# One one-hot product with 128 places per expert, and one shared third tile of down for the leftover tokens

## The chip, the cores and the metric

The kernel runs on one core of one Trainium2 chip. The metric is the device time of one execution in microseconds; it is given as the median of several runs, with the lowest and the highest. One further execution was recorded by the profiler; the rows below come from it.

## The reference, cut to what matters

The program is one block of an encoder: attention and a short convolution on the normed input, added to the residual, then a layer of 16 experts, then a last norm. The change lies in the layer of experts. Each expert chooses its own tokens:

```python
cap = EC_CAPACITY_FACTOR * L // N_EXPERTS           # 2 * 528 // 16 = 66 tokens
g, idx = lax.top_k(aff.T, cap)                      # per expert
xg = hs[idx]                                        # (16, 66, 1024)
a = jnp.einsum('ecd,edf->ecf', xg, w_gate)          # 1024 -> 2048
u = jnp.einsum('ecd,edf->ecf', xg, w_up)
y = jnp.einsum('ecf,efd->ecd', jax.nn.silu(a) * u, w_down)   # 2048 -> 1024
y = y * g[..., None]
out = jnp.zeros((L, D), y.dtype).at[idx.reshape(-1)].add(y.reshape(-1, D))
```

All is float32. The three weight matrices of an expert have 24 MiB together, those of all experts 384 MiB. 66 tokens are 64 and 2 more, and these two are what the change is about.

## The kernel before

After attention and convolution (to about 315 us) and the routing (to about 350 us) comes the loop over experts, L1024 to L1057, in an order written out by hand (`order3`, a manual schedule). Weights are streamed: 384 loads of 1 MiB, issued by SyncE in the order of their use (`pump`, L752) into a ring of 20 buffers (`raw`); `nextw` (L950) takes the oldest buffer for TensorE and issues loads for those that are free.

Expert e has 16 steps of gate and up. A step is 64 matmul instructions on one load (`prod`, L957, weights stationary, the 66 tokens moving; every float32 product is two instructions). After every second step stand two more pieces of work: one piece of to_tokens for the results of expert e-2 (L1038, from the third expert on), and one piece of down for expert e-1 (L1040). So 8 times per expert TensorE does 128 instructions of gate or up, one to_tokens and one `down_piece`.

`down_piece` (L976) takes a load of w_down and multiplies it with the hidden values H (2048 x 66, 16 tiles of 128 x 66), H stationary and weights moving, in four column strips of 32. Three strips hold three groups of tokens, which begin at `GR = (0, 32, 34)`: tokens 0 to 31, 32 to 63 and 34 to 65, so that the third group repeats 30 tokens for the sake of the last two. Groups 0 to 2 are rows 0 to 95 of the three PSUM banks of y (banks 0 and 1); what the fourth strip (rows 96 to 127, one bank per group) gives is the second half of the columns for the odd inner tiles and is added later.

`down_rows` (L989) reads y when an expert's down is complete: ScalarE scales with the gate and rounds to the two-part form's first part (yh, L996), VectorE takes the difference as the second part (yl, L997), ScalarE brings the fourth strip over in three passes (L1000), VectorE adds (L1001), ScalarE and VectorE split again (L1002, L1003). GpSimd makes the one-hot matrix oh (L1005), 96 places x 512 tokens, from the token numbers in `at96`; the repeated 30 places have the number 0 and match nothing.

`to_tokens` (L1008) sends results back to token order with two products, oh times yh and oh times yl, each 96 places x 128 tokens x 512 columns, into the one bank of T, and VectorE adds T to `acc` (L1015).

`at96` is made in the routing: the product with `sel` (L922) spreads numbers and gates of the 66 tokens over 96 places. It stands between the gather of the first expert's rows and `spin(5)`, products without use that TensorE does until the first expert can begin.

PSUM has eight banks. A pool lays its tags into banks in the order in which they are first asked for: in the pool of the loop T has bank 0, G banks 1 and 2, U banks 3 and 4, y banks 5 to 7. The pools of the tail, opened when that pool is closed, lay ys0 and ys1 into banks 0 and 1 and the six places of `bank()` into banks 2 to 7 (in the order 2, 7, 3, 4, 5, 6 as they are asked for). A tile of theirs waits until the tiles that lay in its bank have been read for the last time (`reuse_waits="tile"`).

The tail (from L1059) is no longer in an order by hand: a planner orders the instructions of each engine when the program is built, by their place in the text and by what is ready. The last expert's down runs there with weights stationary: eight steps of 64 instructions into ys0 and ys1 (L1100), each followed by one to_tokens for expert 14 (L1101); then the last expert's own products to token order (L1079), the sums, the last norm and the stores.

## Time and profile before

| | |
|---|---|
| median of 3 runs | 1372.51 us (1372.21 to 1373.56) |
| the profiled execution | 1373.22 us, its span 1371.4 us |
| TensorE busy | 1272.6 us (93% of the span) |
| VectorE, ScalarE, GpSimd busy | 29%, 17%, 13% |
| read from HBM | 427.19 MB, 315 GB/s over the span |
| chain that ended last | TensorE 78%, DMA 7%, VectorE 6% |

The page gives busy times, 40 equal slices of the span, the DMA queues and the chain of work that ended last; further views give the same for any stretch, line or tile. The engines are TensorE (PE; its weight loads into the array stand apart as PEld), VectorE (DVE), ScalarE (ACT), GpSimd (POOL) and SyncE (SP, with its queue SPq). L957 is line 957 of the kernel. A name as y<-raw,H says what is written and what is read.

### The profile page before, as it was taken

The page shows a single profiled execution, that of the slowest core. Times are in us where ns is not written, and L with a number is a line of the kernel's source. Part 1 is how long each engine was busy: PE and PEld are TensorE (multiplying, and loading weights), DVE is VectorE, ACT ScalarE, POOL GpSimd, SP SyncE. Part 2 cuts the span into 40 slices and gives each one's busy share as a digit, 9 for nine tenths or more (in the row PEclk, how much of TensorE's full clock was granted, in tenths as well). Part 3 has the DMA queues.
Part 4 walks back from the last instruction along what each step waited for, and adds up shares of the span by engine and source line. Part 5 has one row for each costly group of instructions (what it writes and reads, how often), then busy time and mean ns, then how long its engine had stood idle before and what let it go on. Part 6 is the DMA issues. An engine that isn't in the chain of part 4 may idle for free.

```text
span 1371.4 us, 47094 instructions
## 1 busy us (share of the span) xinstructions
PE 1272.6 (93%) x22328; PEld 931.3 (68%) x22328; DVE 391.0 (29%) x669; ACT 232.1 (17%) x431; POOL 175.3 (13%) x139
## 2 busy tenths in 40 slices
PE   7897989997879999999999999999999999999996
PEld 6677989995666666666666666666666666565664
DVE  6876776545000111112111112111111111121114
ACT  4455444322000101011010101001010101010112
POOL 2734441331100000000000000000000000000002
PEclk8899889998899999999999999999999999999998
DMA  7311211294999999999999999999999999999994
GB/s 208 93 32 31 62 32 62 94 383 171 337 335 401 396 398 404 391 407 393 406 399 403 385 386 399 392 399 390 399 386 403 393 388 405 382 402 397 407 369 157
DMA packets 142883, 434.51 MB, mean 317 GB/s; under 512 B 13201, under 2 KB 37777, under 8 KB 142689
## 3 DMA queue, kind: packets, MB, share of 16 engines
q1 hardware_dynamic: 139936, 423.49, 80.8%
q0 software_dynamic: 2752, 8.00, 1.9%
q8 instruction: 175, 2.87, 0.9%
q14 instruction: 20, 0.16, 0.0%
HBM read 427.19 MB, written 4.26 MB: 315 GB/s over the span
## 4 chain that ended last, share of the span: by engine, by line
PE 78%; DMA 7%; DVE 6%; issue 4%; ACT 3%; POOL 2%; SPq 0%; DVEq 0%; ACTq 0%; POOLq 0%
PE y L984 21%; PE G L957 17%; PE U L957 17%; PE T L1014 5%; PE pj L274 5%; PE pj L304 3%; DMA raw<-in_w_gate 3%; DMA raw<-in_w_up 3%; PE ys L957 1%; PE pj L344 1%; PE y L986 1%; ACT qsw L365 1%; PE sc L430 1%; PE T L969 1%; ACT p L441 1%
## 5 line engine op out<-in xcount | busy, mean ns | idle before, releaser
L984 PE MATMUL y<-raw,H 128*32 128x512 f32 x2160 | 338.4, 599 | 2.0 <-issue 2.0
L986 PE MATMUL y<-raw,H 128*32 128x512 f32 x720 | 333.6, 599 | 1.5 <-issue 1.5
L957 PEld LDWEIGHTS U<-X,raw 128*64 128x64 f32 x8192 | 249.9, 139 | 66.4 <-issue 51.2
L957 PEld LDWEIGHTS G<-X,raw 128*64 128x64 f32 x8192 | 249.1, 138 | 59.7 <-issue 52.3
L957 PE MATMUL U<-X,raw 128*64 128x66 f32 x8192 | 261.7, 224 | 23.6 <-issue 18.1
L957 PE MATMUL G<-X,raw 128*64 128x66 f32 x8192 | 260.8, 224 | 17.3 <-issue 14.6
L1015 DVE TENSOR_TENSOR acc<-acc,T 128x512 f32<-128x512 f32 x112 | 76.9, 687 | 598.1 <-PE T L1014 598.1
L984 PEld LDWEIGHTS y<-raw,H 128*32 128x32 f32 x2160 | 79.9, 109 | 187.0 <-issue 172.8
L1052 ACT ACTIVATE H<-G 128x264 f32<-128x264 f32 x64 | 21.5, 388 | 595.1 <-PE G L957 595.1
L915 POOL DMA_INDIRECT xg<-hn_rows,idxT x16 | 16.3, 1017 | 699.4 <-PE T L969 680.1
L986 PEld LDWEIGHTS y<-raw,H 128*32 128x32 f32 x720 | 69.4, 110 | 7.0 <-issue 6.9
L274 PE MATMUL pj<-xh,wl 128*128 128x264 f32 x320 | 69.3, 300 | 0.0
L274 PE MATMUL pj<-xl,wh 128*128 128x264 f32 x320 | 67.7, 294 | 0.0
L274 PE MATMUL pj<-xh,wh 128*128 128x264 f32 x320 | 67.2, 293 | 0.0
L996 ACT ACTIVATE yh<-y,at 96x512 fp32r<-96x512 f32 x15 | 10.3, 684 | 281.9 <-PE y L986 281.9
L1014 PE MATMUL T<-yh,oh 96*128 96x512 f32 x112 | 55.8, 498 | 0.0
L274 PEld LDWEIGHTS pj<-xh,wl 128*128 128x128 f32 x320 | 52.9, 201 | 0.1
L274 PEld LDWEIGHTS pj<-xl,wh 128*128 128x128 f32 x320 | 52.5, 199 | 0.0
L274 PEld LDWEIGHTS pj<-xh,wh 128*128 128x128 f32 x320 | 52.2, 198 | 0.0
L1005 POOL TENSOR_SCALAR oh<-tok,at 96x512 fp32r<-96x512 int16 x15 | 23.6, 1573 | 171.4 <-PE T L1014 171.4
L1014 PE MATMUL T<-yl,oh 96*128 96x512 f32 x112 | 44.4, 397 | 0.6 <-issue 0.6
L1054 DVE TENSOR_TENSOR H<-H,U 128x264 f32<-128x264 f32 x64 | 24.4, 423 | 70.8 <-PE U L957 70.8
(226 smaller groups left out, 1201.3 us busy)
## 6 DMA issues: line engine op xcount, KB each, us to landing
raw<-in_w_up SPq DMA_DIRECT2D x128, 1024.0 KB, 18.8
raw<-in_w_gate SPq DMA_DIRECT2D x126, 1024.0 KB, 19.1
raw<-in_w_down SPq DMA_DIRECT2D x126, 1024.0 KB, 19.1
raw<-in_w_in SPq DMA_DIRECT2D x24, 512.0 KB, 5.3
raw<-in_w_out SPq DMA_DIRECT2D x8, 512.0 KB, 4.1
hn_rows<-raw SPq DMA_DIRECT2D x4, 512.0 KB, 4.8
raw<-in_w_gate POOLq DMA_DIRECT2D x2, 1024.0 KB, 8.0
out<-raw SPq DMA_DIRECT2D x4, 512.0 KB, 3.1
```

Of the source, the lines that this page charges most:

```text
L274: nc.tensor.matmul(o[:, hf * 512:hf * 512 + HALF], a[:, c], b[:, HS[hf]], start=c == 0 and n == 0, stop=c == DC - 1 and n == 2)
L304: nc.tensor.matmul(o[:, hf * 512:hf * 512 + HALF], a[:, k, i * P:(i + 1) * P], b[:, HS[hf]], start=k == 0 and n == 0, stop=k == 3 and n == 2)
L344: nc.tensor.matmul(o, a[:, ts], b, start=c == 0 and n == 0, stop=c == DC - 1 and n == 2)
L915: nc.gpsimd.indirect_dma_start(out=xg, out_offset=None, in_=hn2_d, in_offset=bass.IndirectOffsetOnAxis(ap=idxT[:CAP, e:e + 1], axis=0))
L957: nc.tensor.matmul(out[64 * q:64 * q + 64], w[:, c0 + 64 * q:c0 + 64 * q + 64], x, start=first, stop=last, skip_group_check=True)
L984: nc.tensor.matmul(y[32 * g:32 * g + 32, ob], H[:, 2 * d + ci, GR[g]:GR[g] + 32], w[:, o:o + 512], start=d == 0 and r != 1, stop=d == 7 an ...
L986: nc.tensor.matmul(y[96:128, r], H[:, 2 * d + 1, GR[r]:GR[r] + 32], w[:, 1536:2048], start=d == 0, stop=d == 7, skip_group_check=True)
L1005: nc.gpsimd.tensor_scalar(oh, tok, at96[:96, e:e + 1], None, op0=ALU.is_equal)
L1014: nc.tensor.matmul(po, oh[:, t * P:(t + 1) * P], b[:, hfs], start=n == 0, stop=n == 1)
L1015: nc.vector.tensor_tensor(acc[:, t, hfs], acc[:, t, hfs], po, op=ALU.add)
L1052: nc.scalar.activation(dst, src, AF.Silu)
L1054: nc.vector.tensor_tensor(dst, dst, src, op=ALU.mult)
```

## The change

- The two parts of an expert's first 64 tokens become the upper and the lower half of one tile of 128 places (`rows`), so that one product per piece sends both back; oh has 128 places, each token number standing twice (`atp` instead of `at96`).
- The last two tokens of every expert are collected: after each half of gate and up VectorE copies their hidden values into two of the 32 columns of HL (one HL for even, one for odd experts), GpSimd clears those of two experts before. The third group of `down_piece` multiplies HL instead of H. Its rows of y (64 to 95, and the third bank of the fourth strip) are started once, at expert 0, and go on adding over all 15 experts, each expert at its own two rows.
- y is now one tile for the whole loop, asked for before all others of its pool, instead of a new one per expert.
- `down_rows` reads 64 rows of y instead of 96 and has two passes for the fourth strip instead of three. At the end of the loop the shared 32 rows are read once, in the same way (`two_parts`), as a second product (`oh_l`, `rows_l`) for the 8 to_tokens of the tail, which still have two products each.
- In the routing `sel` is made anew, a second product spreads the leftover tokens' numbers and gates over 32 rows of 16 x 2, and `own` picks for each row its own expert's (`atl`).

```diff
@@ -771,12 +769,23 @@
     nc.vector.tensor_scalar(anti, jq, 0.0, None, op0=ALU.is_equal)
 
 
-    jg = hp.tile([P, 3, 32], I32, name="jg")
-    for k in range(3):
-        nc.gpsimd.iota(jg[:, k], pattern=[[-1, 32]], base=-GR[k], channel_multiplier=1)
-    sel = hp.tile([P, 3, 32], F32, name="sel")
-    nc.vector.tensor_scalar(sel, jg, 0.0, None, op0=ALU.is_equal)
-    nc.vector.memset(sel[:, 2, :64 - GR[2]], 0.0)
+
+    sel = hp.tile([P, 3, 64], F32, name="sel")
+    jg = hp.tile([P, 2, 64], I32, name="jg")
+    nc.gpsimd.iota(jg, pattern=[[0, 2], [-1, 64]], base=0, channel_multiplier=1)
+    nc.vector.tensor_scalar(sel[:, 0:2], jg, 0.0, None, op0=ALU.is_equal)
+    jl = hp.tile([P, 32, 2], I32, name="jl")
+    nc.gpsimd.iota(jl, pattern=[[0, 32], [-1, 2]], base=-64, channel_multiplier=1)
+    nc.vector.tensor_scalar(sel[:, 2], jl.rearrange("p a b -> p (a b)"), 0.0, None, op0=ALU.is_equal)
+    own = hp.tile([64, 2, NE], F32, name="own")
+    for k in range(2):
+        jo = hp.tile([32, NE], I32, name=f"jo{k}")
+        nc.gpsimd.iota(jo, pattern=[[-2, NE]], base=0, channel_multiplier=1)
+        jf = hp.tile([32, NE], F32, name=f"jf{k}")
+        nc.vector.tensor_scalar(jf, jo, 0.0, None, op0=ALU.is_ge)
+        nc.vector.tensor_scalar(own[32 * k:32 * k + 32, 0], jo, 2.0, None, op0=ALU.is_lt)
+        nc.vector.tensor_tensor(own[32 * k:32 * k + 32, 0], own[32 * k:32 * k + 32, 0], jf, op=ALU.mult)
+        nc.vector.tensor_copy(own[32 * k:32 * k + 32, 1], own[32 * k:32 * k + 32, 0])
     lg = sc()
 
@@ -918,13 +927,18 @@
 
     xg = gather(0)
 
-    pp96 = pj()
-    nc.tensor.matmul(pp96[:96, :2 * NE], sel[:CAP].rearrange("p a b -> p (a b)"),
+    ppl = pj()
+    nc.tensor.matmul(ppl[:, :2 * NE], sel[:CAP, 0:2].rearrange("p a b -> p (a b)"),
                      vals2[:CAP].rearrange("p a b -> p (a b)"), start=True, stop=True)
+    nc.tensor.matmul(ppl[:64, 512:512 + 2 * NE], sel[:CAP, 2], vals2[:CAP].rearrange("p a b -> p (a b)"),
+                     start=True, stop=True)
     spin(5)
-    at96 = const.tile([P, 2 * NE], F32, name="at96")
+    atp = const.tile([P, 2 * NE], F32, name="atp")
+    atl = const.tile([64, 2], F32, name="atl")
     last = const.tile([P, 2], F32, name="last")
-    nc.vector.tensor_copy(at96[:96], pp96[:96, :2 * NE])
+    nc.vector.tensor_copy(atp, ppl[:, :2 * NE])
+    nc.vector.tensor_tensor(own, own, ppl[:64, 512:512 + 2 * NE].rearrange("p (a e) -> p a e", e=NE), op=ALU.mult)
+    nc.vector.reduce_sum(atl, own, axis=AX.X)
     nc.vector.tensor_copy(last[:CAP], vals2[:CAP, :, NE - 1])
     pump(NRAW, nc.gpsimd)
@@ -941,7 +955,10 @@
     ps2 = psm.enter_context(tc.tile_pool(name="ps2", bufs=1, space=PSUM, reuse_waits="tile"))
     NF = DFF // P
     HS = [wk.tile([P, NF, CAP], F32, name=f"H{i}") for i in range(2)]
-    tok = wk.tile([96, 512], mybir.dt.int16, name="tok")
+    HL = [wk.tile([P, NF, 32], F32, name=f"L{i}") for i in range(2)]
+    for h_ in HL:
+        nc.gpsimd.memset(h_, 0.0)
+    tok = wk.tile([P, 512], mybir.dt.int16, name="tok")
     nc.gpsimd.iota(tok, pattern=[[1, 512]], base=NMETA, channel_multiplier=0)
 
@@ -973,45 +990,62 @@
     def new_x():
         return wk.tile([P, DC, CAP], F32, name="X", tag="X", bufs=2)
 
-    def down_piece(y, H, d):
+    y = ps2.tile([P, 3, 512], F32, name="y")
+
+    def down_piece(e, d):
+
 
 
         w = nextw()
+        H, Hl = HS[e % 2], HL[e % 2]
+
+        def st(f, g):
+            return Hl[:, f] if g == 2 else H[:, f, 32 * g:32 * g + 32]
+
+        def first(g):
+            return d == 0 and (g < 2 or e == 0)
+
+        def final(g):
+            return d == 7 and (g < 2 or e == NE - 2)
+
         for r in range(3):
             ob, ci = ((0, 0), (0, 1), (1, 0))[r]
             o = ci * 1024 + ob * 512
             for g in range(3):
-                nc.tensor.matmul(y[32 * g:32 * g + 32, ob], H[:, 2 * d + ci, GR[g]:GR[g] + 32], w[:, o:o + 512],
-                                 start=d == 0 and r != 1, stop=d == 7 and r != 0, skip_group_check=True)
-            nc.tensor.matmul(y[96:128, r], H[:, 2 * d + 1, GR[r]:GR[r] + 32], w[:, 1536:2048], start=d == 0, stop=d == 7,
+                nc.tensor.matmul(y[32 * g:32 * g + 32, ob], st(2 * d + ci, g), w[:, o:o + 512],
+                                 start=first(g) and r != 1, stop=final(g) and r != 0, skip_group_check=True)
+            nc.tensor.matmul(y[96:128, r], st(2 * d + 1, r), w[:, 1536:2048], start=first(r), stop=final(r),
                              skip_group_check=True)
 
-    def down_rows(y, e):
-
-        gate = at96[:96, NE + e:NE + e + 1]
-        yh = wk.tile([96, D], FR, name="yh", tag="yh")
-        yl = wk.tile([96, D], FR, name="yl", tag="yl")
-        tmp = wk.tile([96, 512], F32, name="tmp", tag="tmp")
-        a, b = slice(0, 512), slice(512, D)
-        nc.scalar.activation(yh[:, a], y[:96, 0], AF.Copy, scale=gate)
-        nc.vector.scalar_tensor_tensor(yl[:, a], y[:96, 0], gate, f32(yh[:, a]), op0=ALU.mult, op1=ALU.subtract)
-        for g in range(3):
+    A, B = slice(0, 512), slice(512, D)
+
+    def two_parts(rows, n, src, src3, gate):
+
+        hi, lo = rows[:n], rows[n:2 * n]
+        nc.scalar.activation(hi[:, A], src[:, 0], AF.Copy, scale=gate)
+        nc.vector.scalar_tensor_tensor(lo[:, A], src[:, 0], gate, f32(hi[:, A]), op0=ALU.mult, op1=ALU.subtract)
+        tmp = wk.tile([64, 512], F32, name="tmp", tag="tmp")[:n]
+        for g, s3 in enumerate(src3):
             gs = slice(32 * g, 32 * g + 32)
-            nc.scalar.activation(tmp[gs], y[96:128, g], AF.Copy, scale=at96[gs, NE + e:NE + e + 1])
-        nc.vector.scalar_tensor_tensor(tmp, y[:96, 1], gate, tmp, op0=ALU.mult, op1=ALU.add)
-        nc.scalar.copy(yh[:, b], tmp)
-        nc.vector.tensor_tensor(yl[:, b], tmp, f32(yh[:, b]), op=ALU.subtract)
-        oh = wk.tile([96, 512], FR, name="oh", tag="oh")
-        nc.gpsimd.tensor_scalar(oh, tok, at96[:96, e:e + 1], None, op0=ALU.is_equal)
-        return oh, yh, yl
+            nc.scalar.activation(tmp[gs], s3, AF.Copy, scale=gate[gs])
+        nc.vector.scalar_tensor_tensor(tmp, src[:, 1], gate, tmp, op0=ALU.mult, op1=ALU.add)
+        nc.scalar.copy(hi[:, B], tmp)
+        nc.vector.tensor_tensor(lo[:, B], tmp, f32(hi[:, B]), op=ALU.subtract)
+
+    def down_rows(e):
+
+        rows = wk.tile([P, D], FR, name="rows", tag="rows")
+        two_parts(rows, 64, y[:64], [y[96:128, 0], y[96:128, 1]], atp[:64, NE + e:NE + e + 1])
+        oh = wk.tile([P, 512], FR, name="oh", tag="oh")
+        nc.gpsimd.tensor_scalar(oh, tok, atp[:, e:e + 1], None, op0=ALU.is_equal)
+        return [(oh, rows)]
 
     def to_tokens(po, rows, d):
 
-        oh, yh, yl = rows
         hf, t = divmod(d, 4)
         hfs = slice(hf * 512, (hf + 1) * 512)
-        for n, b in enumerate((yh, yl)):
-            nc.tensor.matmul(po, oh[:, t * P:(t + 1) * P], b[:, hfs], start=n == 0, stop=n == 1)
+        for n, (oh, b) in enumerate(rows):
+            nc.tensor.matmul(po, oh[:, t * P:(t + 1) * P], b[:, hfs], start=n == 0, stop=n == len(rows) - 1)
         nc.vector.tensor_tensor(acc[:, t, hfs], acc[:, t, hfs], po, op=ALU.add)
 
     order3 = ctx.enter_context(ExitStack())
@@ -1023,7 +1057,6 @@
     rows = None
     for e in range(NE):
         H = HS[e % 2]
-        y = banks("y", 3) if e else None
         i = 0
         for h in range(2):
             for n in range(2):
@@ -1037,7 +1070,7 @@
                     if i % 2 and rows is not None:
                         to_tokens(banks("T", 1)[:, 0], rows, i // 2)
                     if i % 2 and e:
-                        down_piece(y, HS[(e - 1) % 2], i // 2)
+                        down_piece(e - 1, i // 2)
                     i += 1
                     if i in (10, 12) and e + 1 < NE:
                         if i == 10:
@@ -1052,10 +1085,21 @@
                         nc.scalar.activation(dst, src, AF.Silu)
                     else:
                         nc.vector.tensor_tensor(dst, dst, src, op=ALU.mult)
+            if e < NE - 1:
+                hl = HL[e % 2][:, 8 * h:8 * h + 8]
+                if e > 1:
+                    nc.gpsimd.memset(hl[:, :, 2 * e - 4:2 * e - 2], 0.0)
+                nc.vector.tensor_copy(hl[:, :, 2 * e:2 * e + 2], H[:, 8 * h:8 * h + 8, 64:])
         if e:
-            rows = down_rows(y, e - 1)
+            rows = down_rows(e - 1)
         X = Xn
 
+
+    rows_l = moe_raw()[:64, :D].bitcast(FR)
+    oh_l = moe_raw()[:64, :512].bitcast(FR)
+    two_parts(rows_l, 32, y[64:96], [y[96:128, 2]], atl[:32, 1:2])
+    nc.gpsimd.tensor_scalar(oh_l, tok[:64], atl[:, 0:1], None, op0=ALU.is_equal)
+    rows.append((oh_l, rows_l))
     order3.close()
 
     gfin = xgp.tile([P, D], F32, name="xg", tag="xg")
```

## Rows read from the trace of the kernel before

**Rows 1.** The page: span, and busy time of TensorE with its share.

```profile
span 1371.4 us, 47094 instructions
PE 1272.6 (93%) x22328; PEld 931.3 (68%) x22328; DVE 391.0 (29%) x669; ACT 232.1 (17%) x431; POOL 175.3 (13%) x139
```

**Rows 2.** Sums by window; columns: busy times, granted clock, DMA share, GB/s.

```profile
354.00:421.00 67.00, 54.17 (x1432) 47.51 (x1432) 2.40 (x6) 3.30 (x7) 0.98 (x1) 0.92 0.97 355
421.00:721.00 300.00, 290.64 (x6074) 192.20 (x6068) 45.24 (x79) 23.47 (x45) 12.88 (x10) 1.00 1.03 400
721.00:1021.00 300.00, 290.08 (x6016) 191.99 (x6016) 47.47 (x83) 22.80 (x43) 12.91 (x10) 0.99 1.02 393
1021.00:1341.00 320.00, 307.04 (x6318) 201.57 (x6312) 50.63 (x87) 23.46 (x45) 13.06 (x10) 1.00 1.02 394
```

**Rows 3.** Line L752, first 400 to 440 us, then 1140 to 1200 us.

```profile
L752 SPq DMA_DIRECT2D raw<-in_w_up x7: 367/368/368, 400.9 to 438.2; - x7
DMA to landing us min/median/max: 5.6/9.2/11.5
...
L752 SPq DMA_DIRECT2D raw<-in_w_up x6: 409/2306/2745, 1142.3 to 1176.7; - x6
DMA to landing us min/median/max: 18.1/19.2/23.2
```

**Rows 4.** Timeline of GpSimd: start and length of the one-hot matrix per expert.

```profile
518.97 1.57 POOL L1005 TENSOR_SCALAR oh<-tok,at 96x512 fp32r<-96x512 int16 x1 [10.66 <-PE T L1014]
...
1011.30 1.57 POOL L1005 TENSOR_SCALAR oh<-tok,at 96x512 fp32r<-96x512 int16 x1 [12.48 <-PE T L1014]
...
1135.11 1.57 POOL L1005 TENSOR_SCALAR oh<-tok,at 96x512 fp32r<-96x512 int16 x1 [11.20 <-PE T L1014]
...
1265.73 1.57 POOL L1005 TENSOR_SCALAR oh<-tok,at 96x512 fp32r<-96x512 int16 x1 [13.53 <-PE T L1014]
```

**Rows 5.** Waits of PEld, 1121 to 1331 us: in total, times, longest (us).

```profile
PEld U L957 <- DMA raw<-in_w_up: 10.7, 12, 2.7
```

**Rows 6.** Timeline of one unit: two products to tokens, down, then gate.

```profile
701.46 0.50 PE L1014 MATMUL T<-yh,oh 96*128 96x512 f32 x1
...
701.80 0.40 PE L1014 MATMUL T<-yl,oh 96*128 96x512 f32 x1
...
702.13 0.63 PE L984 MATMUL y<-raw,H 128*32 128x512 f32 x3
...
704.84 3.96 PE L957 MATMUL G<-X,raw 128*64 128x66 f32 x128
```

**Rows 7.** Timeline of the tail, from the end of the last down_piece.

```profile
1330.78 2.09 PE L957 MATMUL ys<-H,raw 128*64 128x66 f32 x64
1330.94 0.68 ACT L996 ACTIVATE yh<-y,at 96x512 fp32r<-96x512 f32 x1 [17.52 <-PE y L986]
1331.66 0.75 DVE L997 SCALAR_TENSOR_TENSOR yl<-y,at,yh 96x512 fp32r<-96x512 f32 x1 [2.12 <-ACT yh L996]
1332.44 2.07 ACT L1000 ACTIVATE tmp<-y,at 32x512 f32<-32x512 f32 x3 [0.82 <-DVE yl L997]
...
1334.55 0.75 DVE L1001 SCALAR_TENSOR_TENSOR tmp<-y,at,tmp 96x512 f32<-96x512 f32 x1 [2.14 <-ACT tmp L1000]
...
1335.33 0.62 ACT L1002 CAST yh<-tmp 96x512 fp32r<-96x512 f32 x1 [0.81 <-DVE tmp L1001]
...
1353.77 1.95 PEld L957 LDWEIGHTS ys<-H,raw 128*64 128x64 f32 x64 [0.35 <-issue]
```

**Rows 8.** A pause in the first expert, and the window around it (clock: 0.51).

```profile
397.92 2.80 PE L957 MATMUL U<-X,raw 128*64 128x66 f32 x46 [3.89 <-issue]
...
397.00:404.00 7.00, 6.08 (x112) 6.08 (x114) 0.77 (x2) 0.00 (x0) 0.00 (x0) 0.51 0.83 298
```

**Rows 9.** Timeline of the routing's end: the selecting product and its copy.

```profile
343.46 0.53 PE L922 MATMUL pj<-vals,sel 66*96 66x32 f32 x2 [1.02 <-DVE vals L911]
...
344.02 0.19 DVE L927 COPY at<-pj 96x32 f32<-96x32 f32 x1 [0.62 <-PE pj L922]
```

More of the change, by code (lines that the diff above doesn't have):

```diff
@@ L40 @@
 RING = (6, 6, 3, 5)
-GR = (0, 32, 34)
 NRAW = sum(RING)
```

## The prediction

> **What bounds the kernel now.** The page comes first: TensorE is busy for 93% of the span [rows 1], so it looks like the bound, and the change takes work from it. The question is whether that time is worth anything in the expert loop, so I read the loop by stretches, weight stream beside TensorE. In the sums by window [rows 2] the reader is to see that from 421 to 1341 us the DMA share stays at 1.02 to 1.03 and the rate at 393 to 400 GB/s, while before it, in the first expert, the rate was 355. Then the issues of the weight loads at L752 [rows 3]: early (400 to 440 us) an issue takes 0.37 us and a load lands 9.2 us later; late (1140 to 1200 us) an issue takes 2.31 us and landing takes 19.2 us. More and more loads stand in line, and the rate does not rise with them: the stream runs at its limit from some 421 us on.
>
> An expert needs 24 loads of 1 MiB, 25.17 MB. At 400 and 394 GB/s [rows 2] that is 62.9 and 63.9 us. TensorE's pace is read from the one-hot mask that GpSimd makes once per expert (L1005) [rows 4]: from 518.97 to 1011.30 us eight experts pass, 61.5 us each; from 1135.11 to 1265.73 us two pass, 65.3 us each. So for most of the loop TensorE is 1.5 to 2.5 us per expert faster than the stream and lives on the stock of 20 weight buffers that was filled before the loop. After some 1130 us the stock is gone: in 1121 to 1331 us TensorE's loads from these buffers wait 10.7 us for landings of w_up alone [rows 5]. The last 200 us are already paced by the stream, and with them the end.
>
> **The change part by part.** (a) One product fewer per to_tokens. In one unit the first product begins at 701.46, the second at 701.80, the first matmul of down at 702.13 us [rows 6]: the removed one is worth 0.33 us. The loop calls to_tokens 8 times for each of 14 experts (112 calls; the 8 calls of the tail keep two products, the second now being the shared tile's). That is 112 x 0.33 = 37 us of TensorE, 2.6 us per expert, and the pace becomes 61.5 - 2.6 = 58.9 us against a stream of 63 to 64. The stock, which lasted from the third expert (460 us) to 1130 us, is now used up at about twice the rate, so it ends near 800 us, and from there TensorE waits for the stream. The first to_tokens comes in the third expert, when the stream is already at its limit, so no load is issued to any use earlier. I count this at 0: what hides it is the stream, the same one that ends the loop in both kernels. If that cover were gone, it would be worth the whole 37 us.
>
> (b) Work added to the loop: two small copies of H's last two columns per expert on VectorE, two small clears on GpSimd. Nothing of this size is in the trace; the nearest rows are the copy of 32 elements at 0.19 us [rows 9] and the 512-element operations at 0.75 us [rows 7], so two copies (of 16 elements a partition) cost 0.4 to 1.5 us, nearer 0.4, on an engine with 45 of 300 us busy [rows 2]. The shared columns are read one expert later. One ScalarE pass of 0.69 us per expert goes [rows 7]. All of it lies under the new slack of 64 - 58.9 = 5 us per expert, from both sides 0.
>
> (c) Routing, ahead of the loop. One more selecting product: the present one (L922) holds TensorE for 0.53 us at most [rows 9], its end overlapping the warm-up products behind it, and these are followed by the first transpose, so it is on the path: between 0 and 0.5, I take 0.3. The extra VectorE operations behind L927 run beside the warm-up products. Some ten tiny VectorE and GpSimd operations stand before the routing; bounded by 0.2 us each (the copy at L927 took 0.19) [rows 9] they cost 0 to 2 us, and I take 0, as they need nothing that is late. A later first expert shifts the stream and the end by as much; a luckier or unluckier first expert could move the end by 2 us either way.
>
> (d) The tail, where I see the price. The new y is asked for ahead of T, so it takes the first three banks; the last expert's sums ys0 and ys1 are laid in the first two banks again. In the kernel before these banks belonged to T and G, free early, and ys began at 1330.78 us, while down was still ending [rows 7]. Now ys0 must wait until y has been read for the last time, and that is at the end of a chain which the change makes longer. By the rows of before [rows 7]: down ends about 1330.85; the scaling pass on ScalarE runs 1330.94 to 1331.62, the difference on VectorE to 1332.41, then ScalarE's passes over the fourth strip. These are two instead of three, 1.38 us, to 1333.82; the sum on VectorE 0.75, to 1334.61; ScalarE's copy 0.62, to 1335.26. Only then the shared tile: scaling 0.68, to 1336.03; strip 0.69, to 1336.8 (the difference, 0.75, runs beside it); sum 0.75, to 1337.6, and y is free. ys0 starts at 1337.7 instead of 1330.78: 6.9 us later. In before TensorE has no pause worth naming from here to the last ys block, which begins at 1353.77 us [rows 7], so a late start is a late end: the loads meanwhile land and wait.
>
> What can run in the gap: products of to_tokens for part 1 to 3 (the first takes bank 2, also y's), which the planner, free to reorder after order3.close(), may pull ahead: 3 x 2 x 0.33 = 2.0 us back; 0 if it doesn't, 5.3 if all eight go. And TensorE's clock: after a pause of 3.89 us in the first expert 46 matmuls took 2.80 us, 61 ns each, and the clock granted in 397 to 404 us was 0.51 [rows 8], the lower level of 1.2 GHz, against 31 ns (128 in 3.96 us) at full clock [rows 6]. A gap of 6.9 us with little in it will do the same. A drop costs between 0 and 3.5 us (half of those 7 us); I take 2.5, nearer to that row than to none.
>
> Sum: 0.3 + 6.9 - 2.0 + 2.5 = +7.7 us. The profiled execution took 1373.22 us, 1.8 more than its span of 1371.4 [rows 1], and becomes 1380.9; the median of the runs, 1372.51, lies 0.7 under the profiled one, so the forecast is 1380.2. The bounds together, from 0.3 + 6.1 - 5.3 + 0 = +1 (ys0 waits for the reads of its own bank alone) to 2 + 7.6 + 0 + 3.5 = +13 (strip behind difference), give 1373.5 to 1385.5; both ends at once are unlikely, and 1376 to 1384 is the forecast's own range.
>
> A rule speaks for a gain. The Trainium skill, Perfetto Trace Analysis, section Engine Utilization, puts the practical ceiling of a single busy core at about 120% of 358 GB/s, limited by its 16 DMA engines at some 435. By that the stream would have 8% in hand: at 430 an expert's loads would take 58.5 us (an estimate from that page) and TensorE's 58.9 would decide. The trace disagrees: with landing times doubled the rate did not pass 400 [rows 2, 3].
>
> **The rivals.** First, the stream is no limit and TensorE's 37 us come back: 1372.5 - 37 + 7.7 = 1343, or part of it. For it speaks 93% busy TensorE; against it that the rate is flat while the line grows, and that TensorE waits for landings at the end. 5%. Second, the other side of the forecast, not slower: the same mechanism in the tail has no price, because ys0 doesn't wait for the shared tile (other banks, or other work put there in full). It decides at the point where y's last read ends before 1331 us or 6.9 us of ready work exist; then the end stays with the stream, 1372.5 + 0.3, within 2 us: 1373. For it: the stream ends the loop at the same time and nothing else in the tail is changed; against it: only some 2 to 5 us of ready products exist. 21%. Third, the copies and clears of the shared tile stall TensorE by more than the 5 us per expert that are free: 15 x (stall - 5); with 6 us, 15 us more, 1395. Nothing in VectorE's or GpSimd's load speaks for it. 3%. The forecast has 71%.
>
> **How the numbers follow.** The range runs from 1373 to 1384.5: it takes in the forecast's own range, its upper bound nearly, and half of the second rival. About 0.2% (2.7 us) is what a measurement of this kernel can tell from no change. Faster: the first rival and a little of a lucky first expert, 0.07. Same: nearly all of the second and the foot of the forecast, 0.21. Slower: 0.72.
>
> **What would show it.** In the loop: single T products at L1014's successor, 112 fewer TensorE products, mask-to-mask times near 59 us at first and near 64 to 65 us from about 800 us on, with waits of TensorE for raw that begin there and add up to some 37 us more than before; the same rate of 393 to 400 GB/s and a last landing within 1 us of before. In the tail: ys0's first matmul 6 to 8 us after down's end, released by VectorE's last sum on y, and a granted clock under 1.00 in the stretch after it. Wrong would be: a loop that ends earlier than 1325 us (the stream was no limit), or ys0 right behind down (no price in the tail).

## The result, and the profile after

| | before | after |
|---|---|---|
| median of four runs each | 1372.55 us (1372.21 to 1373.56) | 1385.26 us (1381.73 to 1387.8) |
| ratio | | 1.009 (95% interval 1.0066 to 1.0113): slower by 0.9% |
| profiled execution, span | 1371.4 us | 1386.0 us |
| first product of expert 0 | 352.2 | 354.4 |
| end of down for expert 14 | 1330.85 | 1333.34 |
| first product of ys | 1330.78 | 1340.85 |
| first product of the last ys block | 1353.77 | 1368.18 |

Times in the last four rows are microseconds from the start of the profiled execution; that of after is the slowest of its four. The forecast was 1380.2 with a range to 1384.5: the right sign and place, 5 us too little, and 0.8 us outside the range.

The page of after, span, busy times and the chain that ended last, to set beside [rows 1]:

```profile
span 1386.0 us, 46951 instructions
PE 1260.5 (91%) x22218; PEld 923.7 (67%) x22218; DVE 404.7 (29%) x712; ACT 223.7 (16%) x419; POOL 180.4 (13%) x169
...
PE 62%; DMA 22%; DVE 7%; issue 4%; ACT 3%; POOL 1%; SPq 0%; DVEq 0%; ACTq 0%; POOLq 0%
```

TensorE has less to do, and the time goes up; DMA's share of the chain has risen from 7 to 22%. The stretches of [rows 2] in after (busy times, granted clock, DMA share, GB/s):

```profile
421.00:721.00 300.00, 287.24 (x6061) 189.08 (x6058) 48.22 (x89) 20.06 (x40) 13.68 (x19) 1.00 1.02 399
721.00:1021.00 300.00, 287.80 (x6059) 189.58 (x6054) 51.67 (x94) 19.38 (x38) 13.83 (x20) 1.00 1.02 393
1021.00:1341.00 320.00, 287.50 (x5937) 187.94 (x5938) 51.69 (x92) 21.63 (x43) 15.26 (x18) 0.99 1.02 393
```

The rate is the same to 1 GB/s, and TensorE is busy for 20 us less in the last stretch (7.5 of them are a gap in the tail, shown below). What became of its removed work is in the waits of its weight loads from 460 to 1331 us (in total, times, longest), first before, then after:

```profile
PEld U L957 <- DMA raw<-in_w_up: 10.7, 12, 2.7
PEld y L984 <- DMA raw<-in_w_down: 5.1, 14, 0.4
PEld G L957 <- DMA raw<-in_w_gate: 4.6, 8, 1.1
```

```profile
PEld U L974 <- DMA raw<-in_w_up: 24.3, 27, 2.5
PEld y L1015 <- DMA raw<-in_w_down: 10.4, 28, 0.9
PEld G L974 <- DMA raw<-in_w_gate: 10.2, 19, 1.0
```

With the smaller rows of the same view, waits for landings rose from 28.5 to some 51 us: 23 us of new waiting. From the first product of expert 0 to the end of down it is 978.6 us before and 979.0 after.

The tail of after, from the end of the last down_piece (start, length, what it does, in brackets the idle time before it and who ended it); it answers [rows 7]:

```profile
1333.45 0.68 ACT L1025 ACTIVATE rows<-y,atp 64x512 fp32r<-64x512 f32 x1 [17.55 <-PE y L1017]
1334.17 0.74 DVE L1026 SCALAR_TENSOR_TENSOR rows<-y,atp,rows 64x512 fp32r<-64x512 f32 x1 [2.25 <-ACT rows L1025]
...
1338.50 0.75 DVE L1026 SCALAR_TENSOR_TENSOR raw<-y,atl,raw 32x512 fp32r<-32x512 f32 x1
1339.28 0.68 ACT L1030 ACTIVATE tmp<-y,atl 32x512 f32<-32x512 f32 x1 [0.82 <-DVE raw L1026]
1340.00 0.74 DVE L1031 SCALAR_TENSOR_TENSOR tmp<-y,atl,tmp 32x512 f32<-32x512 f32 x1 [0.75 <-ACT tmp L1030]
...
1340.85 3.99 PE L974 MATMUL ys<-H,raw 128*64 128x66 f32 x64 [7.49 <-DVE tmp L1031]
```

The last row holds the mechanism that was forecast, ys waiting 7.49 us for VectorE's last sum on y, and its consequence: 3.99 us for a block that took 2.09 before. The two stretches behind it show the clock at its lower level, 1.2 GHz:

```profile
1336.00:1343.00 7.00, 2.15 (x37) 2.12 (x39) 3.60 (x5) 2.92 (x5) 0.00 (x0) 0.55 1.04 375
1343.00:1350.00 7.00, 7.00 (x100) 5.88 (x96) 0.69 (x1) 0.00 (x0) 0.00 (x0) 0.50 0.62 229
```

### The profile page after: what moved, and what is told of

It is laid out like the page before. It is cut to its first block, busy times and chain, and to the rows that moved or that the text cites. A ratio compares the mean times of both kernels' runs of the same rounds, so it can differ in the third digit from the quotient of the medians.

```text
span 1386.0 us, 46951 instructions
## 1 busy us (share of the span) xinstructions
PE 1260.5 (91%) x22218; PEld 923.7 (67%) x22218; DVE 404.7 (29%) x712; ACT 223.7 (16%) x419; POOL 180.4 (13%) x169
## 3 DMA queue, kind: packets, MB, share of 16 engines
q8 instruction: 174, 2.85, 0.9%
## 4 chain that ended last, share of the span: by engine, by line
PE 62%; DMA 22%; DVE 7%; issue 4%; ACT 3%; POOL 1%; SPq 0%; DVEq 0%; ACTq 0%; POOLq 0%
PE y L1015 16%; PE G L974 13%; PE U L974 13%; DMA raw<-in_w_gate 9%; DMA raw<-in_w_up 7%; DMA raw<-in_w_down 5%; PE pj L272 4%; PE pj L302 3%; PE T L1048 2%; PE ys L974 1%; PE pj L342 1%; ACT qsw L363 1%; PE sc L428 1%; DVE wl L232 1%; ACT p L439 1%
## 5 line engine op out<-in xcount | busy, mean ns | idle before, releaser
L1015 PE MATMUL y<-raw,H 128*32 128x512 f32 x1440 | 335.8, 596 | 6.7 <-DMA raw<-in_w_down 2.2
L1015 PE MATMUL y<-raw,L 128*32 128x512 f32 x720 | 333.2, 596 | 3.1 <-issue 3.1
L974 PE MATMUL U<-X,raw 128*64 128x66 f32 x8192 | 264.9, 224 | 30.9 <-issue 18.2
L1017 PE MATMUL y<-raw,H 128*32 128x512 f32 x480 | 229.6, 599 | 0.2 <-issue 0.2
L1015 PEld LDWEIGHTS y<-raw,H 128*32 128x32 f32 x1440 | 73.9, 109 | 174.5 <-issue 157.8
L1017 PE MATMUL y<-raw,L 128*32 128x512 f32 x240 | 122.6, 592 | 0.0
L1015 PEld LDWEIGHTS y<-raw,L 128*32 128x32 f32 x720 | 68.8, 109 | 8.5 <-issue 8.4
L1048 PE MATMUL T<-rows,oh 128*128 128x512 f32 x112 | 56.1, 501 | 0.7 <-issue 0.7
L1025 ACT ACTIVATE rows<-y,atp 64x512 fp32r<-64x512 f32 x15 | 10.2, 682 | 280.5 <-PE y L1017 280.5
L1017 PEld LDWEIGHTS y<-raw,H 128*32 128x32 f32 x480 | 42.5, 109 | 5.7 <-issue 5.7
```

The lines of the kernel that those rows point to most:

```text
L974: nc.tensor.matmul(out[64 * q:64 * q + 64], w[:, c0 + 64 * q:c0 + 64 * q + 64], x, start=first, stop=last, skip_group_check=True)
L1015: nc.tensor.matmul(y[32 * g:32 * g + 32, ob], st(2 * d + ci, g), w[:, o:o + 512], start=first(g) and r != 1, stop=final(g) and r != 0, ski ...
L1017: nc.tensor.matmul(y[96:128, r], st(2 * d + 1, r), w[:, 1536:2048], start=first(r), stop=final(r), skip_group_check=True)
L1048: nc.tensor.matmul(po, oh[:, t * P:(t + 1) * P], b[:, hfs], start=n == 0, stop=n == len(rows) - 1)
```

## The experiments

Each time stands beside the kernel before as run with it on the same chip (1372.7, 1373.6 and 1373.5 us in the three groups of four). Two lengths from each profile carry most of the argument: the loop, from the first product of expert 0 to the end of the last down, and the tail, from there to the end of the span. In microseconds (loop and tail from one profile each, the time a median; after itself was run only beside the first kernel before, at 1372.55):

| kernel | loop | tail | time |
|---|---|---|---|
| before | 978.6 | 40.6 | 1372.55 |
| after | 979.0 | 52.6 | 1385.26 |
| before, one product in the loop | 978.9 | 41.2 | 1374.89 |
| after, y in banks 5 to 7 | 980.1 | 48.9 | 1382.06 |
| the same, shared product later | 977.2 | 46.1 | 1379.67 |
| after, with filler | 976.4 | 50.1 | 1383.19 |
| after, routing moved | 979.8 | 49.7 | 1385.69 |
| after, padded | 976.7 | 48.1 | 1381.75 |
| shared rows ride | 978.3 | 40.6 | 1376.15 |
| shared rows ride, mended | 976.9 | 42.2 | 1374.33 |
| before / after, 20 loads | 951.1 / 946.5 | 38.4 / 50.0 | 1344.93 / 1350.64 |
| before / after, 12 loads | 922.5 / 894.0 | 38.8 / 49.9 | 1313.37 / 1302.67 |

### What the removed product is worth

```diff
-        for n, b in enumerate((yh, yl)):
+        for n, b in enumerate((yh, yl)[:parts]):
...
-                        to_tokens(banks("T", 1)[:, 0], rows, i // 2)
+                        to_tokens(banks("T", 1)[:, 0], rows, i // 2, 1)
```

> The kernel before, whose to_tokens inside the loop does only the first of its two products (the tail keeps both); the second parts of experts 0 to 13 are left out of the result. It takes away the work that the change takes from TensorE, and nothing else of the change. Theory (the stream paces the loop): the time stays at 1372.5 within 1.5 us, and the waits for landings in the loop grow. Rival (TensorE paces it): 112 x 0.23 to 0.33 us come back, 1335 to 1347 us.

1374.89 us, ratio 1.0013 (1.0003 to 1.0023). The removal alone gives nothing, if anything it costs a little; the loop is as long as before and its waits for landings are 51 us, as in after. TensorE's work in the loop is not what paces it. The loops of the ten kernels with 24 loads lie between 976.4 and 980.1 us with no order by the change, so differences of 2 us between single profiles say nothing.

Is it the stream? Two pairs make the stream lighter and leave TensorE's work alone: the first with every second load of down used twice, the second with every second load of gate and up as well. Of their edits only the uses are shown, not the order of the loads:

```diff
-        w = nextw()
+        w = held[0] = nextw() if d % 2 == 0 else held[0]
...
-                    w = nextw()
+                    w = nextw() if k % 2 == 0 else w
```

> The kernel before with a lighter stream: of each expert's eight w_down loads in the loop only the even ones are made and each is used for two pieces (half of down's weights of experts 0 to 14 are left out of the result), 20 loads per expert instead of 24; at 396 GB/s that is 53 us. TensorE's work is unchanged. Theory: TensorE now paces the loop with some 61 us per expert to the end, and no expert takes 65 us: down ends near 1317 us instead of 1331, the time is about 1358 to 1361 us. Rival (the stream had no part in the pace): 1372.

> The changed kernel with the same lighter stream as the kernel before had in its light version. Theory: with the stream out of the way the removed products do come back, 112 x 0.23 to 0.33 = 26 to 37 us in the loop, less the 12 us that the tail and the 2 us that the routing cost: 1335 to 1347 us, so 12 to 25 us under the light version of before. Rival (the removed products were hidden by something else than the stream, TensorE's own stalls or the copies): no gain, 1370 us or more.

1344.93 and 1350.64 us. The kernel before gained more than I had reckoned, so the stream does set its pace; but the changed kernel was 5.7 us slower than its partner, which neither theory gave: its loop was only 4.6 us shorter instead of 26 to 37. The waits of TensorE from 460 to 1230 us, first before, then after, both with 20 loads:

```profile
PE U L957 <- issue: 6.9, 8, 1.5
PE G L957 <- issue: 3.9, 6, 1.4
...
```

```profile
PE U L974 <- issue: 11.0, 12, 2.0
PE G L974 <- issue: 6.8, 5, 2.3
PE y L1017 <- issue: 5.4, 7, 1.2
```

"Issue" is a wait for nothing that this view shows; its rows sum to 13.1 us before and 25.4 after. Three stretches at the lower clock (from 609, 756 and 1268 us, each right behind a pause of 1.8 to 2.0 us) took after some 5 us more. So of the 26 us, 4.6 came, 12.3 went to pauses, some 5 to the clock, and some 4 stay without a name. One such pause in after with 20 loads, in the timeline of TensorE, and the DMA queues' packets, megabytes and share from 606.2 to 607.4 us:

```profile
603.06 3.72 PE L974 MATMUL G<-X,raw 128*64 128x66 f32 x120
608.64 0.45 PE L974 MATMUL G<-X,raw 128*64 128x66 f32 x8 [1.85 <-issue]
...
609.55 1.07 PE L1017 MATMUL y<-raw,H 128*32 128x512 f32 x2
```

```profile
q1 hardware_dynamic: 126, 0.47, 98.8%
q8 instruction: 1, 0.02, 5.6%
```

TensorE stops in the middle of a block whose load has long landed. In just this stretch a packet of instructions comes in; TensorE goes on 1.3 us after its end. The page of after counts this queue:

```profile
q8 instruction: 174, 2.85, 0.9%
```

2.85 MB in 174 packets are 16 KB each, and 2 x 22218 instructions of TensorE [the page above] over 174 packets are 255 for each. Of this kernel's 26 pauses of over 0.3 us from 460 us on, all but two (the gap of the tail, and the last transposition) end 1.3 to 1.6 us after such a packet, and these lie at the same place in a count by 256 of the recorded instructions (the place drifts slowly, since some records are missing). So I read these pauses as TensorE waiting for its own instructions, which come through the same 16 DMA engines as the weights. If that is so, they must go when the engines have room:

> The kernel before with half of all its weight loads in the loop: of gate and up too only every second load is made and used twice (half of all expert weights of the loop are left out of the result). 12 loads per expert, some 210 GB/s. In the light version (350 GB/s) TensorE still paused 0.3 to 1.5 us at a time, each time at the same place in a run of 256 of its instructions and 1.3 to 1.5 us after a 16 KB packet of instructions had landed. Theory (the instructions come through the same DMA engines as the weights and come late when these are full): with the engines half empty the pauses go, an expert takes 58.8 us instead of 60.4, the time falls from 1344.9 to some 1322 to 1328 us. Rival (the pauses do not depend on the weights): 1344 us again.

> The changed kernel with the same half of the loads. Theory: without pauses the removed products come back in full: 0.23 us (from 0.66 to 0.43 us between to_tokens' first product and down) x 112 = 26 us in the loop, less some 12 us for the tail; 57 us per expert, 1309 to 1315 us, some 14 us under the kernel before with the same loads (the light pair went the other way: 1350.6 against 1344.9). Rival (the pauses belong to TensorE's own supply of instructions, whatever the weights do): about 1349 us, not faster than its partner.

1313.37 and 1302.67 us (two runs each, 4 us apart): lower than I had put either, and 10.7 apart with the changed kernel ahead, against 14 expected. The stretch from 460 to 1230 us of both, then the waits of TensorE in it (before, after):

```profile
460.00:1230.00 770.00, 767.74 (x16099) 508.70 (x16097) 127.54 (x221) 60.98 (x117) 34.71 (x27) 1.00 0.64 218
...
PE G L957 <- issue: 1.4, 2, 1.2
PE U L957 <- issue: 0.6, 2, 0.4
```

```profile
460.00:1230.00 770.00, 767.85 (x16552) 512.59 (x16549) 138.78 (x252) 52.14 (x104) 37.07 (x52) 1.00 0.64 218
...
PE y L1017 <- issue: 0.8, 1, 0.8
PE U L974 <- issue: 0.7, 1, 0.7
PE G L974 <- issue: 0.3, 1, 0.3
```

At a DMA share of 0.64 the pauses are gone (2.0 and 1.8 us left), TensorE is busy throughout, and the loops differ by 28.5 us: from the first to_tokens product to down it is 0.66 us before and 0.43 after, and 112 x 0.23 = 26. So the removed work is real, and it showed in full only here, where neither the weights nor the instructions come late. A rule speaks on this: the Trainium skill, Runtime: NRT & Kernel Launch, section Instruction fetch mechanics, has the 16 KiB blocks of 256 instructions and calls crossing a block's boundary "mostly hidden". With the DMA engines two thirds busy the trace agrees; with them full it does not (25.4 us in 770).

### The tail: one chain, waited for in three places

```diff
-    y = ps2.tile([P, 3, 512], F32, name="y")
...
+        if e == 1:
+            y = ps2.tile([P, 3, 512], F32, name="y")
```

> The changed kernel with the shared y asked for at expert 1, after T, G and U, so that it lies in banks 5 to 7 as before and ys0, ys1 lie under T and G. If the bank under ys0 were the whole price of the tail, the gap of 7.5 us and the low clock behind it would go: 1373 to 1375 us. Theory: the same chain is waited for once more, by the first to_tokens, which needs the shared rows; the first block of ys moves into the gap (2 us), TensorE then stands for some 6 us before the first to_tokens, and the clock falls all the same: 1382 to 1384 us.

1382.06 us. The bank under ys0 is free, and the next instruction waits instead:

```profile
1335.67 2.09 PE L974 MATMUL ys<-H,raw 128*64 128x66 f32 x64
1337.69 0.50 PE L1046 MATMUL bk<-rows,oh 128*128 128x512 f32 x1
1341.78 0.76 PE L1046 MATMUL bk<-raw 64*128 64x512 f32 x1 [3.58 <-DVE raw L1024]
1342.47 3.79 PE L974 MATMUL ys<-H,raw 128*64 128x66 f32 x64
```

The shared product needs the shared rows, 3.58 us later, and the clock falls all the same (0.54 from 1345 to 1352 us). What was gained is the block and the product that now stand in the gap, 2.5 us, and a low stretch of 10.2 instead of 13.7 us. Next, the shared product is moved as well:

```diff
-    rows.append((oh_l, rows_l))
...
-        to_tokens(bank(), rows, i)
+        to_tokens(bank(), rows + [(oh_l, rows_l)] * (i > 3), i)
...
+        if hf == 0:
+            nc.tensor.matmul(po[t, hf], oh_l[:, t * P:(t + 1) * P], rows_l[:, :512], start=False, stop=True)
```

> As the kernel with y in banks 5 to 7, and the product of the shared tile is done later: for the first half of the columns beside the last expert's own products to token order (behind the seventh block), for the second half in the to_tokens of blocks 5 to 8. Nothing in the first half of the tail needs the shared rows then. Theory (the chain behind down is the price): both waits are gone, and with them gap and low clock; what is left is the later end of down (2.5 us in the profiled run): 1373 to 1376 us. Rival (the loop itself has become slower, by the calls that stall in it): 1381 us or more, since nothing in the loop is changed.

1379.67 us, between theory and rival. The loop was no longer than before (977.2), so the rival is out; the tail was still 5.5 us longer, for a reason that I had not seen:

```profile
1338.64 0.40 PE L1046 MATMUL bk<-rows,oh 128*128 128x512 f32 x1 [2.96 <-DVE tmp L1029]
1338.97 3.50 PE L974 MATMUL ys<-H,raw 128*64 128x66 f32 x64
```

The second place of `bank()` is bank 7, which is y's in this layout, and waits for the same last read of y; then one slow block, and the shared products themselves. Moving a tile to other banks only moved the wait to the next tile that is laid over it.

The low clock by itself: TensorE is given work without use for the time of the gap.

```diff
     rows.append((oh_l, rows_l))
+    junk = banks("G", 2)
+    for k in range(8):
+        nc.tensor.matmul(junk[:, k % 2], ident, X[:].rearrange("p a b -> p (a b)")[:, :512], start=True, stop=True)
```

> The changed kernel with eight products without use (128 x 128 x 512, 0.85 us each, 6.8 us) written behind the last down_piece, so that TensorE is busy while it would wait 7.5 us for the shared tile's chain. Nothing else moves: ys0 waits for the same read. Theory (the low clock behind the gap costs 4 to 5 us, two blocks of 3.9 us instead of 2.1 and some more): 1380 to 1381.5 us, with a granted clock of 1.00 in the stretch. Rival (the clock costs nothing because the loads or the vector work decide there): 1385 us as before the edit.

1383.19 us, 2.1 less than after instead of the 4 to 5 expected; as after's own four runs lie 6 us apart, the rows tell more than the times.

```profile
1331.23 7.13 PE L1105 MATMUL G<-X,ident 128*128 128x512 f32 x16
1338.79 2.09 PE L974 MATMUL ys<-H,raw 128*64 128x66 f32 x64 [0.42 <-PE G L1105]
...
1341.66 1.62 PE L974 MATMUL ys<-H,raw 128*64 128x66 f32 x48
1344.93 0.69 PE L974 MATMUL ys<-H,raw 128*64 128x66 f32 x16 [1.65 <-issue]
```

The block takes 2.09 us and the granted clock is 1.00 from 1338 to 1345 us, so the clock stayed up and the expected 4.4 us were won there (in after two blocks and the pair between them took 9.1 us instead of 4.9, and the product behind them 0.6 instead of 0.43); 1.65 us went to a pause for instructions in the next block. After's median may hold less than the whole 4.4 us: in the padded and the routing version, with the same gap (7.49 and 7.48 us), the low stretch was half as long (6.8 us, not 13.7). That may be part of why after's runs lie 6 us apart; the runs that weren't profiled don't show it.

The pair of products in the tail took longer than before's:

```diff
-    rows_l = moe_raw()[:64, :D].bitcast(FR)
-    oh_l = moe_raw()[:64, :512].bitcast(FR)
+    rows_l = moe_raw()[:, :D].bitcast(FR)
+    oh_l = moe_raw()[:, :512].bitcast(FR)
+    nc.gpsimd.memset(f32(rows_l[64:]), 0.0)
+    nc.gpsimd.memset(f32(oh_l[64:]), 0.0)
```

> The changed kernel, its shared rows and their one-hot matrix padded with zeros from 64 to 128 places, so that both products of a pair in the tail have 128 rows. If the change from 128 to 64 rows is what makes the pair take 0.85 us (0.66 in the kernel before, 96 and 96 rows), the pair falls to 0.66 to 0.7 us and the tail gets 1.2 to 1.5 us shorter; if it is the second stationary matrix (in the kernel before both products of a pair load the same one), it stays at 0.85.

1381.75 us (two runs). A pair and the next block, first in after, then padded:

```profile
1352.99 0.50 PE L1048 MATMUL bk<-rows,oh 128*128 128x512 f32 x1
1353.42 0.49 PE L1048 MATMUL bk<-raw 64*128 64x512 f32 x1
1353.84 2.09 PE L974 MATMUL ys<-H,raw 128*64 128x66 f32 x64
```

```profile
1348.30 0.50 PE L1048 MATMUL bk<-rows,oh 128*128 128x512 f32 x1
1348.63 0.39 PE L1048 MATMUL bk<-raw 128*128 128x512 f32 x1
1348.95 2.09 PE L974 MATMUL ys<-H,raw 128*64 128x66 f32 x64
```

0.85 us become 0.65, though the second product has twice the rows: it was the change of rows from 128 to 64. Eight pairs make 1.6 us. The tail is 4.5 us shorter than after's, and the rest of that goes with the shorter low clock: against the routing version, whose low stretch is as short, it is 1.6 us shorter (49.7 and 48.1).

### Ahead of the loop

```diff
-    nc.tensor.matmul(ppl[:64, 512:512 + 2 * NE], sel[:CAP, 2], vals2[:CAP].rearrange("p a b -> p (a b)"),
-                     start=True, stop=True)
...
-    nc.vector.reduce_sum(atl, own, axis=AX.X)
...
+        if e == 2:
+            leftovers()
```

`leftovers` holds the same operations with names of its own.

> The changed kernel with only the small operations for the leftovers' numbers and gates (second product with sel, own, atl) moved from ahead of the loop to expert 2. If they cost 2 us ahead of the first expert, the first expert begins 2 us earlier (near 352.3) and the time is 1383.3; if the later start in the profiled run was chance, the time stays at 1385 and the first expert starts anywhere between 352 and 355.

1385.69 us, first expert at 354.3: no gain in either. But the scatter of the start hides one. TensorE's product that begins at 248.90 us in before and at 249.70 in after, long before the routing, begins anywhere from 248.6 to 252.3 us in the fourteen profiles, and here at 250.79. From it to the first product of expert 0 it is 103.3 to 103.6 us in the four kernels made from before, 104.6 to 106.3 in the seven with the small operations ahead of the loop (104.66 in after), and 103.5 to 104.0 in the three that have them at expert 2. So these operations, the second selecting product among them, cost 1.3 us in after and up to 3.0 elsewhere; the other 0.8 of after's later start (2.1) is the scatter before that product. More than half of the 1.3 us arises at one place, at a product of attention with `aTa`, first in before, then in after:

```profile
255.26 0.27 PE L480 MATMUL tr<-aTa,vl 112*128 112x224 f32 x1
```

```profile
255.03 1.29 DVE L785 TENSOR_SCALAR jf<-jo 32x16 f32<-32x16 int32 x1
256.25 0.56 DVE L470 TENSOR_TENSOR aTb<-tr,aTb 112x400 fp32r<-112x400 f32 x1
...
256.86 0.37 PE L478 MATMUL tr<-aTa,vl 112*128 112x224 f32 x1 [0.66 <-DVE aTb L470]
```

One of the small operations, on 32 x 16 elements, took 1.29 us (why, no run shows); VectorE's difference `aTb` stood behind it, and TensorE waited for that. This product comes 0.8 us later after the one at 249 us in all seven kernels, and not in the three others. From the router's last product on, the way to expert 0 is 32.21 us after and 31.87 before: 0.34 for the second selecting product. How much of it reaches the end isn't decided: the two kernels with 24 loads and the longest way (106.3; with filler and padded) have two of the shortest loops (976.4 and 976.7), and in this version TensorE waited 5.5 us at expert 2 for the operations moved there.

### A version without the prices

y lies in banks 4 to 6, which the tail takes last, and the shared rows take the unused rows of the last expert's products:

```diff
+    early_gu = {k: banks(k, 2) for k in "GU"}
     y = ps2.tile([P, 3, 512], F32, name="y")
...
+        R = slice(96, 128)
+        h0, l0, h1, l1 = (yraw[R, k * 512:(k + 1) * 512] for k in range(4))
+        g, src = lastx[R, 1:2], y[64:96]
+        nc.scalar.activation(h0, src[:, 0], AF.Copy, scale=g)
```

> A version meant to keep the single product and take away each price found. (1) G, U, then y, then T are asked for, so y lies in banks 4 to 6, which the tail takes last. (2) The shared rows get no product of their own: their two parts lie in rows 96 to 127 of the last expert's two operands (66 rows before, 128 now), their tokens in the same one-hot matrix, so by_token sends both back. (3) The small operations for the leftovers' numbers and gates stand in the loop at expert 2. Theory: down ends as before near 1331, no wait for y, eight single products instead of pairs in the tail (8 x 0.23 = 1.8 us less), so the last block is reached when its load lands (1350 us) rather than at 1353.8: 1369 to 1372 us, up to 3 us under the kernel before. Rival (the changed loop itself costs, 1 to 2 us as the kernel of before with one product suggests at 1374.9): 1373 to 1376 us.

1376.15 us, ratio 1.002 (1.0011 to 1.0029); then with the wait at expert 2 taken out:

> The version whose shared rows ride with the last expert's own products, with one thing mended: the small operations for the leftovers' numbers and gates are begun at the start of expert 2 and their product stands five steps later, so that TensorE no longer waits 5.5 us for them there. Theory (the stream sets the end of the loop): that wait was hidden, the time stays at 1376 us within 1.5. Rival (stock lost early counts at the end): 1371 to 1373 us.

1374.33 us, ratio 1.001 (0.9999 to 1.0021): level with before. It came 1.8 us under the first version, neither theory's number, and the profiled runs start 2.5 us apart, so the small question (does lost stock count at the end) isn't decided. The larger one is: the tail's price is gone (tails of 40.6 and 42.2 us, 40.6 before). The gain of eight single products, 1.8 us, isn't there either, and the tail of the mended version shows where it went:

```profile
1336.87 2.09 PE L958 MATMUL ys<-H,raw 128*64 128x66 f32 x64 [1.18 <-issue]
...
1343.08 0.27 PE L958 MATMUL ys<-H,raw 128*64 128x66 f32 x1 [1.68 <-issue]
```

Two pauses, 2.9 us, each ending 1.3 us after a packet of instructions, in the stretch in which the last weights still fill the DMA engines (before had one of 0.7). Behind the second the clock was at its lower level for 3.4 us, which it wasn't in the first version, with pauses of the same length; that goes with the 1.6 us between the two tails. The change, mended, has nothing to give here.

## Why the prediction was too low

- **The loop is worth 0.** Right in its result and, for the kernel as it is, in its reason: same rate, same loop, 23 us of new waits for landings, and nothing gained by the removal alone. Two sizes were off. The product is worth 0.23 us, not the 0.33 between two starts [rows 6], since a product alone takes longer than one of a pair: 26 us, not 37. And the stock lasted to about 1015 us, not 800, because TensorE's pace became 60.8 us per expert (from 522 to 1008 us) and not 58.9. The product's smaller worth makes 59.7 of it, 0.4 us more of waiting per expert makes 60.1, and the rest has no name. The step "if that cover were gone, it would be worth the whole" was wrong for a somewhat lighter stream; beneath the weights lay a second limit, the instructions, which I hadn't looked at.
- **Routing, +0.3, and the small operations, 0.** The second selecting product was right: 0.34. The small operations failed: I took 0, "as they need nothing that is late", and bounded each by 0.2 us. But others stand behind them: one took 1.29 us, TensorE waited, and 1.0 us was lost up to the router's last product in after.
- **ys late, +6.9.** The mechanism was right to the releasing instruction; measured 7.49, as ScalarE's last strip waited for the difference on VectorE (0.82) that I had laid beside it, though in [rows 7] the strips wait for the difference too.
- **Products pulled into the gap, -2.0.** Failed: none was pulled, in any version; the tail kept the order block, products, block. In after the pair contains the shared product, which needs the rows that the gap is waiting for. That isn't the whole reason: where the shared product stood later, TensorE still did nothing from 1335.7 to 1338.6 us rather than go past the waiting product.
- **Low clock, +2.5.** Too small for the profiled run (4.4 us), near in the padded one (its first block 3.49 us instead of 2.09, so 1.4).
- **The tail's pairs.** I counted them as before's: 0.85 instead of 0.66 us, +1.5, a term that wasn't in the sum.
- **"No pause worth naming" in before's tail.** There were some 1.4 us of short ones, which after's tail lacks: one of 0.70 us, and blocks of 2.43 and 2.24 us that take 2.09 and 1.97 elsewhere.

With these the profiled tail is 7.5 + 0 + 4.4 + 1.5 - 1.4 = 12.0 us longer, as measured (52.6 and 40.6). The 2.1 us of the later start and 0.4 in the loop make it 14.5 of the span's 14.6. The medians differ by 12.7; whether the runs without a profile had the shorter low stretch isn't known. So the place and the chain were right, and the sum failed in its small terms: 2.0 us were taken off for products that never moved, 1.5 for the pairs were missing, and the small operations stood at 0 instead of 1.0. That the forecast came within 5 us owes something to before's pauses, which worked the other way.

The rival without a price in the tail fell for this kernel, as y's last read ended at 1340.74 and nothing was pulled ahead; it holds for the version in which the shared rows ride. The third, stalls by copies and clears, isn't to be seen in the loops.

## What to carry to other kernels

Work taken from an engine pays only down to the next supply that is late; look for the second one beneath the first (here the instructions under the weights) by making the first lighter for both kernels, not by reading busy shares. A result gathered over a whole loop puts its whole epilogue at the loop's end: before the text is changed, list everything that will stand in line for it, by data and by the place that it occupies, since removing one wait shows the next. The same goes for small operations ahead of it: count what stands behind them on their engine, not their own length alone. Rows that have no product of their own are best put where a product has rows free.

## What the hardware showed that I had not expected

- TensorE's instructions come in packets of 16 KB through the DMA engines that bring the weights. At a DMA share of 0.95 it paused for them 13.1 us in 770 in the kernel before and 25.4 in the changed one; at 0.64 some 2 us of pauses were left in either.
- A pause of 1.85 us in full work was followed by the lower clock: the y products behind it took 1.07 us instead of 0.60, until about 612 us. Another, of 2.26 us at 795 us in the same profile, was not (granted clock 1.00).
- A pair of products with 128 and 64 rows took 0.85 us, one with 128 and 128 rows 0.65.
- An operation of VectorE on 32 x 16 elements took 1.29 us at one place and 0.15 at another, and TensorE waited behind it.
